# Hybrid DeltaNet and Conformer trunk: filling units, the split of u and gated products at the end of the delta stage

## Chip, core and metric

The kernel runs on one core of a Trainium2 chip. The metric is the device time of one execution in microseconds (us). Engines are named as in the profile: PE (TensorE, matrix products), PEld (its weight loads), DVE (VectorE), ACT (ScalarE), POOL (GpSimd) and SP (SyncE, which here only issues DMAs). Each engine takes its instructions strictly in the order in which they stand in its queue.

## What is computed

Two layers of a sequence model on x of shape 1 x 2048 x 1024. Cut to what matters here, each layer does this:

```
h    = rms_norm(x)
proj = h @ w_in                      # q, k, v, z_a, a, b, cf_val, cf_glu, z_b, gate logits
o    = gated delta rule, chunked, forwards and backwards over the sequence (q, k, v, decay, beta)
y_a  = (norm(o) * silu(z_a)) @ w_dn_out
u    = silu(layer_norm(conv31(cf_val * sigmoid(cf_glu)))) * silu(z_b)
y_b  = u @ w_cf_out
gate = sigmoid(gate_logits + gate_b)          # one 1024-wide gate for each branch
x    = x + (gate[0] * y_a + gate[1] * y_b) @ w_out
```

## The kernel before

Tokens lie along the free axis, channels on the partitions. Every dense product is made of fp32 values split in a high and a low half (`split`: ACT copies the high half, DVE subtracts it to get the low half), so one step over 128 input channels is three matmuls of 128x512 (L174, L175, L176). Call these three a **unit**. Weights are loaded by SP (`wraw`) and split in the same way (`whi`, `wlo`).

A layer has three parts. First come the projections, the convolutions and everything else that needs only h. Then comes the **delta stage** (`delta`): 16 steps, each of which advances the forward and the backward recurrence by one chunk of 128 tokens. Its products are small and each depends on the last, so between them `pull(n)` puts n units of work that does not depend on the recurrence, taken from the generator `filler`: 32 groups of 8 units that make the gate logits of the second half of the sequence (`gates(1)`), and then 64 units, in 16 groups of 4, that make y_b for the first half (`early_merge`). That is 320 units. `LEAD` says how many are pulled before step 0, `STEP` how many at the four places of a step, `TAIL` how many at three places after the last step; what is left then runs with nothing between. Then comes the **merge** (`merge`): for each half of the sequence, 8 channel tiles j by 2 token blocks b, the gated sum of both branches and then the product with w_out.

Within a step, in written order: L967 and L970 (key and query against the state, forward lane, then backward lane), L972 (DVE) and L976 (ACT), pull, L983, L985 (ACT), pull, L992 and L1001, the state update L995 and the output L1003 (both DVE), pull, `finish` of the previous pair of chunks, pull. `finish` (from step 8 on) normalises two output chunks: squares L1022 on ACT, a chain of tiny DVE operations that ends with L1036, the scaling L1040 on ACT, four transposes for each chunk on PE (L1045), L1046 on DVE, and the store to `og`. `prep` prepares the small triangular inverses of later steps (L895 to L950). PSUM tiles called pz come from a ring of five, those called pd (dense products) from a ring of three: who wants one waits until its last user is done.

Within the delta stage the order on PE, ACT, DVE and POOL is the written one (`bind`). Elsewhere, and on SP, a scheduler places instructions, and it also brings some of the merge's first work forward into the end of the delta stage.

u is loaded when unit 239 is done (8 loads, in the low halves' place), and split into its halves at the units that `SPLITS` names. The merge of the first half waits for the last `finish`: its `og` goes to DRAM, comes back as `gop`, and is split.

Of the kernel before, what the change touches and what calls it, by code (L numbers as in the profile page):

```python
# [6 lines left out]
F32 = mybir.dt.float32  # L7
F32R = mybir.dt.float32r
I32 = mybir.dt.int32
AF = mybir.ActivationFunctionType  # L10
ALU = mybir.AluOpType
# [3 lines left out]
P = 128  # L15
L = 2048
HALF = 1024
NB = 512
D = 1024
KD = 8  # L20
# [5 lines left out]
R1 = 3.0  # L26
R3 = 4.5
GAP = 0
SPLITS = [250, 251, 252, 253]
LEAD = (8, 10, 6, 6, 6, 4)  # L30
STEP = (5, 4, 4, 4)
TAIL = (3, 3, 3)
Z = '121'
LATE = 4
AHEAD = 4
# [22 lines left out]
def sort(ps):  # L58
    return ps.rearrange("p (i a) -> p a i", a=2)


def cut(x):
    return x.rearrange("p (a i) -> p a i", a=2)
# [13 lines left out]
class Trunk:  # L77
# [734 lines left out]
    def delta(self):  # L812
# [240 lines left out]
        def pull(n):  # L1053
            for _ in range(n):
                if next(fill, GAP) == GAP:
                    return
# [28 lines left out]
        for step in range(NCH):  # L1085
# [12 lines left out]
            next(last)  # L1098
            pull(STEP[0])
            for x in lanes:  # L1100
# [3 lines left out]
            go(step + 1)  # L1104
            pull(STEP[1])
            for x in lanes:
# [6 lines left out]
            next(new)  # L1113
            pull(STEP[2])
            next(last)
            ready = go(step + 1)
            last = new
            pull(STEP[3])
            ins = nxt
        for n in TAIL:  # L1120
            pull(n)
# [5 lines left out]
    def filler(self):  # L1127
        wcf = self.a["w_cf"][self.l]
        u = None
        for n, v in enumerate(self.gates(1)):  # L1130
            yield v
            if n == 30 * KD - 1:
                self.drain()
                self.rate = 0.0
                u = self.big([P, 8, HALF], F32R, "uop")
                raw = lambda k, b: u[:, 4 + k, b * NB:(b + 1) * NB]
                for b in range(2):
                    for k in range(4):
                        self.load(raw(k, b).bitcast(F32), self.u_d[k, :, b * NB:(b + 1) * NB])
            if n == 31 * KD - 1:  # L1140
                ahead = self.weight(wcf[0], 4)
            if n in SPLITS:
                k = SPLITS.index(n)
                self.split(u[:, k, 0:NB], raw(k, 0), raw(k, 0).bitcast(F32))
        self.u0 = u
        self.t1 = self.big([P, KD, HALF], F32, "t1")
        yield from self.early_merge(wcf, ahead, raw)

    def early_merge(self, wcf, ahead, raw):
        nc = self.nc  # L1150
        for j in range(KD):
            wc = ahead
            if j + 1 < KD:
                ahead = self.weight(wcf[j + 1], 4)
            for b in range(2):
                sl = slice(b * NB, (b + 1) * NB)
                ps = self.pd()
                for k, more in enumerate(self.dense_steps(ps, wc, lambda k: (self.u0[:, k, sl], self.u0[:, 4 + k, sl]), 4)):
                    if j == 0 and b == 0:
                        self.split(self.u0[:, k, NB:HALF], raw(k, 1), raw(k, 1).bitcast(F32))  # L1160
                    if more:
                        yield 1
                nc.scalar.activation(cut(self.t1[:, j, sl]), sort(ps), AF.Copy)
                yield 1

    def operand_parts(self, src, half, name):
        t = self.big([P, 8, HALF], F32R, name)
# [16 lines left out]
    def merge(self, l, xd, fnw):  # L1184
        nc, a = self.nc, self.a
        v_ = nc.vector
        last = l == self.depth - 1
        if not last:
            xnew = self.drm.tile([KD, P, L], F32, name=f"x{l + 1}")
            nvec = self.pv.tile([P, NV], F32, tag="vec", name="vec")  # L1190
            self.load(nvec, a["vecs"][l + 1])
        self.nh = [None] * 4
        prev = None
        wcol = lambda k: nvec[:, V_NW + k:V_NW + k + 1]
        for half in range(2):
            if half == 0:
                og, piece = self.operands(self.og_d, 0, "gop")
                for k in range(4):
                    piece(k)
            yhi = self.big([P, KD, HALF], F32R, "yhi")  # L1200
            ylo = self.big([P, KD, HALF], F32R, "ylo")
            for j in range(KD):
                wc = self.weight(a["w_cf"][l, j], 4) if half else None
                wd = self.weight(a["w_dn"][l, j], 4)
                for b in range(2):
                    sl = slice(b * NB, (b + 1) * NB)
                    tk = slice(half * HALF + b * NB, half * HALF + (b + 1) * NB)
                    gt = self.hm("gt")[:, 0:2 * NB].rearrange("p (n t) -> p n t", n=2)
                    self.load(gt, self.gt_d.rearrange("(n j) p t -> j p n t", n=2)[j][:, :, tk])
                    nc.scalar.activation(gt, gt, AF.Sigmoid)  # L1210
                    y = [gt[:, 0, :], gt[:, 1, :]]
                    if half:
                        ps = self.pd()
                        self.dense(ps, wc, lambda k: (u[:, k, sl], u[:, 4 + k, sl]), 4)
                        v_.tensor_tensor(out=cut(y[1]), in0=sort(ps), in1=cut(y[1]), op=ALU.mult)
                    else:
                        v_.tensor_tensor(out=y[1], in0=self.t1[:, j, sl], in1=y[1], op=ALU.mult)
                    ps = self.pd()
                    self.dense(ps, wd, lambda k: (og[:, k, sl], og[:, 4 + k, sl]), 4)
                    v_.tensor_tensor(out=cut(y[0]), in0=sort(ps), in1=cut(y[0]), op=ALU.mult)  # L1220
                    v_.tensor_tensor(out=y[0], in0=y[0], in1=y[1], op=ALU.add)
                    self.split(yhi[:, j, sl], ylo[:, j, sl], y[0])
            ahead = iter(())
            if half == 0:
                u, pu = self.operands(self.u_d, 1, "uop")
                og, pg = self.operands(self.og_d, 1, "gop")
                ahead = (f(k) for f in (pu, pg) for k in range(4))
            if last:
                self.last_out(l, half, xd, fnw, yhi, ylo, ahead)
                continue  # L1230
            w = self.weight(a["w_out"][l, 0], KD)
            norm = self.normalise(0, *prev, wcol) if prev is not None else iter(())
            xn = []
            for j in range(KD):
                next(ahead, None)
                if half and j == AHEAD:
                    self.scalar_weights(l + 1)
                for _ in range(2 if j % 2 == 0 else 0):
                    next(norm, None)
                if j < 6 and j % 2 == 0:  # L1240
                    t = self.mid("xn")
                    xn += [t[:, 0:HALF], t[:, HALF:2 * HALF]]
                elif j >= 6:
                    xn.append(self.hm("xnh")[:, 0:HALF])
                if j == 0:
                    ss = self.hm("ss")[:, 0:HALF]
                for b in range(2):
                    sl = slice(b * NB, (b + 1) * NB)
                    tk = slice(half * HALF + b * NB, half * HALF + (b + 1) * NB)
                    ps = self.pd()  # L1250
                    self.dense(ps, w, lambda k: (yhi[:, k, sl], ylo[:, k, sl]), KD)
                    xr = self.st("xr")
                    self.load(xr, xd[j][:, tk])
                    v_.tensor_tensor(out=cut(xn[j][:, sl]), in0=sort(ps), in1=cut(xr), op=ALU.add)
                    self.add_square(ss[:, sl], xn[j][:, sl], j == 0)
                    self.store(xnew[j, :, tk], xn[j][:, sl])
                if j + 1 < KD:
                    w = self.weight(a["w_out"][l, j + 1], KD)
            if half:
                continue  # L1260
            r = self.norm_stats(ss)
            prev = (xn, r)
        if last:
            return None, None
        self.ready = 2
        self.lead = self.late_norm(xn, ss, wcol)
        self.vec = nvec
        nh = self.nh
        return nh, [xnew[k] for k in range(KD)]
# [94 lines left out]
```

## Time and profile before

| | |
|---|---|
| device time, median of 3 runs | 3219.36 us (3217.04 to 3219.66) |
| the profiled execution's own time | 3223.96 us |
| its span in the trace | 3222.2 us |
| PE matmuls busy | 3101.0 us, 96% |
| DVE busy | 2401.9 us, 75% |
| ACT busy | 1393.5 us, 43% |
| POOL busy | 302.2 us, 9% |

The profiled execution was 4.6 us longer than the median of the runs, and 1.8 us of its time lie outside the span. The end of a matmul in the trace is modelled, and matmuls overlap, so that a busy PE may still be held up inside a group. The share is an average: where the remaining PE time is lost has to be looked up stage by stage. The delta stage of the first layer lies at about 900 to 1300 us, its merge of the first half behind it up to about 1365; in the second layer they lie at about 2475 to 2874 and 2883 to 2937.

### The profile page before, as it was taken

The numbers are of one execution on the slowest core, as the hardware profiler recorded it, in microseconds if no ns is written. First come the engines' busy times: TensorE is split into PE (matmuls) and PEld (weight loads), VectorE is DVE, ScalarE is ACT, GpSimd is POOL, SyncE is SP. The second block draws the span as 40 slices with busy tenths as digits, with TensorE's granted clock in tenths as the row PEclk, the third lists the DMA queues.
The fourth block names the chain that finished last, engine by engine and source line by source line (L and its number), as shares of the span: only waits on it lengthen the run. The fifth ranks groups of instructions, "written<-read, shape, count | busy, mean of one in ns | idle before, by whom it ended". The sixth has DMA issues, their size and how long they took to land. (4 is left out here: it accounts for less than half of the span.)

```text
span 3222.2 us, 51090 instructions
## 1 busy us (share of the span) xinstructions
PE 3101.0 (96%) x19110; PEld 2711.5 (84%) x19110; DVE 2401.9 (75%) x4409; ACT 1393.5 (43%) x3104; POOL 302.2 (9%) x297
## 2 busy tenths in 40 slices
PE   6999999999999999799999999999999999989997
PEld 5788888888889998687888888888888999877786
DVE  7789898987555687645666989898955567867655
ACT  5625252522344466533345242425234445655332
POOL 3000000000022231000000000000002122200000
PEclk9999999999999999899999999999999999999999
DMA  4233232334687785654413131314358777856644
GB/s 139 88 96 94 84 100 78 102 108 132 215 289 231 261 270 174 191 187 128 141 50 107 66 116 62 119 59 122 116 188 269 236 254 246 265 155 208 206 128 147
DMA packets 427030, 501.67 MB, mean 156 GB/s; under 512 B 95712, under 2 KB 260192, under 8 KB 426784
## 3 DMA queue, kind: packets, MB, share of 16 engines
q1 hardware_dynamic: 354032, 388.58, 38.9%
q10 hardware_dynamic: 64688, 80.09, 7.1%
q0 software_dynamic: 8064, 29.76, 2.4%
q8 instruction: 150, 2.46, 0.3%
q14 instruction: 96, 0.79, 0.1%
HBM read 342.74 MB, written 155.58 MB: 155 GB/s over the span
## 5 line engine op out<-in xcount | busy, mean ns | idle before, releaser
L174 PE MATMUL pd<-h,whi 128*128 128x512 f32 x2816 | 1091.7, 388 | 0.0
L176 PE MATMUL pd<-h,wlo 128*128 128x512 f32 x2816 | 1071.3, 380 | 2.3 <-DVE wlo L158 2.3
L175 PE MATMUL pd<-h,whi 128*128 128x512 f32 x2816 | 1072.1, 381 | 0.0
L728 DVE SCALAR_TENSOR_TENSOR cacc<-gp,vec,cacc 128x1009 f32<-128x1009 f32 (+1 forms) x480 | 615.5, 1282 | 37.8 <-ACT cacc L726 34.7
L174 PEld LDWEIGHTS pd<-h,whi 128*128 128x128 f32 x2816 | 534.6, 190 | 79.3 <-issue 1.4
L176 PEld LDWEIGHTS pd<-h,wlo 128*128 128x128 f32 x2816 | 534.4, 190 | 79.5 <-DVE wlo L158 3.9
L175 PEld LDWEIGHTS pd<-h,whi 128*128 128x128 f32 x2816 | 534.5, 190 | 72.9 <-issue 1.9
L157 ACT ACTIVATE whi<-wraw 128x512 fp32r<-128x512 f32 x400 | 243.0, 624 | 488.6 <-PE pd L175 346.6
L158 DVE TENSOR_TENSOR wlo<-wraw,whi 128x512 fp32r<-128x512 f32 x400 | 279.7, 713 | 175.8 <-ACT whi L157 163.9
L553 DVE SCALAR_TENSOR_TENSOR acc<-cin,vec,acc 128x1022 f32<-128x1022 f32 (+1 forms) x192 | 246.9, 1300 | 14.7 <-ACT acc L551 13.6
L176 PE MATMUL pd<-yhi,wlo 128*128 128x512 f32 x512 | 195.3, 381 | 8.0 <-DVE wlo L158 7.9
L174 PE MATMUL pd<-yhi,whi 128*128 128x512 f32 x512 | 194.7, 380 | 1.4 <-ACT whi L157 1.3
L175 PE MATMUL pd<-ylo,whi 128*128 128x512 f32 x512 | 194.0, 379 | 0.0
L808 ACT ACTIVATE go<-pd,vec 128x512 f32<-128x512 f32 x128 | 87.0, 680 | 133.2 <-PE pd L176 122.6
L529 ACT ACTIVATE cin<-pd 128x512 f32<-128x512 f32 x96 | 57.0, 593 | 156.3 <-PE pd L176 156.1
L174 PE MATMUL pd<-gop,whi 128*128 128x512 f32 x256 | 99.9, 392 | 20.5 <-ACT gop L157 19.3
L176 PEld LDWEIGHTS pd<-yhi,wlo 128*128 128x128 f32 x512 | 96.7, 189 | 25.6 <-DVE wlo L158 12.2
L174 PE MATMUL pd<-uop,whi 128*128 128x512 f32 x256 | 102.9, 402 | 12.8 <-ACT uop L157 7.1
L1210 ACT ACTIVATE gt<-gt 128x1024 f32<-128x1024 f32 x64 | 67.6, 1058 | 108.1 <-DMA gt<-gt 98.9
L740 ACT ACTIVATE ao<-pd 128x512 f32<-128x512 f32 x64 | 38.3, 598 | 170.0 <-PE pd L176 169.9
L976 ACT ACTIVATE dm<-pz,eg 128x128 f32<-128x128 f32 x240 | 68.5, 368 | 98.8 <-PE pz L970 93.7
L174 PEld LDWEIGHTS pd<-yhi,whi 128*128 128x128 f32 x512 | 96.8, 189 | 16.4 <-ACT whi L157 3.0
(296 smaller groups left out, 4837.0 us busy)
## 6 DMA issues: line engine op xcount, KB each, us to landing
wraw<-w_in SPq DMA_DIRECT2D x240, 256.0 KB, 3.2
gt<-go ACTq DMA_DIRECT2D x128, 256.0 KB, 3.4
dl<-gr SPq DMA_DIRECT2D x128, 256.0 KB, 5.1
dl<-kq SPq DMA_DIRECT2D x64, 512.0 KB, 5.9
dl<-kv SPq DMA_DIRECT2D x64, 512.0 KB, 5.2
gt<-gt SPq DMA_DIRECT2D x64, 512.0 KB, 5.0
wraw<-w_out SPq DMA_DIRECT2D x96, 256.0 KB, 3.0
kq<-acc SPq DMA_DIRECT2D x16, 1024.0 KB, 5.5
```

The source lines that it names most:

```text
L157: self.nc.scalar.activation(hi, src, AF.Copy)
L158: self.nc.vector.tensor_tensor(out=lo, in0=src, in1=hi.bitcast(F32), op=ALU.subtract)
L174: mm(ps, whi[:, k, :], xhi, start=k == 0, stop=False)
L175: mm(ps, whi[:, k, :], xlo, start=False, stop=False)
L176: mm(ps, wlo[:, k, :], xhi, start=False, stop=k == kk - 1)
L529: nc.scalar.activation(cut(t[:, o + b * NB:o + (b + 1) * NB]), sort(ps), AF.Copy)
L553: self.nc.vector.scalar_tensor_tensor(out=out, in0=t[:, k:k + n], scalar=wc(k), in1=out, op0=ALU.mult, op1=ALU.add)
L728: self.nc.vector.scalar_tensor_tensor(out=acc, in0=t[:, k:k + n], scalar=wc(k), in1=acc, op0=ALU.mult, op1=ALU.add)
L740: nc.scalar.activation(cut(o), sort(ps), func)
L808: nc.scalar.activation(cut(o), sort(ps), AF.Identity, bias=self.vec[:, V_GB + j:V_GB + j + 1])
L976: nc.scalar.activation(hv(o1)[:, hd, :], pq[:, hd, :], AF.Copy, scale=eg[:, hd:hd + 1])
L1210: nc.scalar.activation(gt, gt, AF.Sigmoid)
```

## The change

Three things. (1) A step pulls 16 units instead of 17 and the three places of TAIL 3, 3, 2, so that 16 units run after the last transposes. (2) u is split at units 247 to 254, one 512-wide piece at each, both token blocks; before, the first block was split at 250 to 253 and the second in the first group of `early_merge`. (3) `early_merge` no longer stores y_b alone (ACT copy, `t1`): it loads the gate of its own tile and block one group ahead, takes the sigmoid on ACT, and DVE writes gate times product to `y1`. The merge of the first half then loads one gate instead of two, and loses a DVE product for each tile and block.

```
-SPLITS = [250, 251, 252, 253]
+SPLIT = 247
-STEP = (5, 4, 4, 4)
-TAIL = (3, 3, 3)
+STEP = (4, 4, 4, 4)
+TAIL = (3, 3, 2)
...
-            if n in SPLITS:
-                k = SPLITS.index(n)
-                self.split(u[:, k, 0:NB], raw(k, 0), raw(k, 0).bitcast(F32))
+            if SPLIT <= n < SPLIT + 8:
+                b, k = divmod(n - SPLIT, 4)
+                self.split(u[:, k, b * NB:(b + 1) * NB], raw(k, b), raw(k, b).bitcast(F32))
...
+        def gate(i):
+            j, b = seq[i]
+            t = self.st("g1")
+            self.load(t, self.gt_d[8 + j][:, b * NB:(b + 1) * NB])
+            return t
+        nxt = gate(0)
+        for i, (j, b) in enumerate(seq):
...
+            g = nxt
+            if i + 1 < len(seq):
+                nxt = gate(i + 1)
+            nc.scalar.activation(g, g, AF.Sigmoid)
...
-                nc.scalar.activation(cut(self.t1[:, j, sl]), sort(ps), AF.Copy)
+            nc.vector.tensor_tensor(out=cut(self.y1[:, j, sl]), in0=sort(ps), in1=cut(g), op=ALU.mult)
...
-                    self.load(gt, self.gt_d.rearrange("(n j) p t -> j p n t", n=2)[j][:, :, tk])
-                    nc.scalar.activation(gt, gt, AF.Sigmoid)
-                    y = [gt[:, 0, :], gt[:, 1, :]]
+                    n = 1 + half
+                    self.load(gt[:, 0:n], self.gt_d.rearrange("(n j) p t -> j p n t", n=2)[j][:, 0:n, tk])
+                    nc.scalar.activation(gt[:, 0:n], gt[:, 0:n], AF.Sigmoid)
+                    y = [gt[:, 0, :], gt[:, 1, :] if half else self.y1[:, j, sl]]
...
-                    else:
-                        v_.tensor_tensor(out=y[1], in0=self.t1[:, j, sl], in1=y[1], op=ALU.mult)
```

The change moves instructions. On PE, at the end of the first layer's delta stage, the last transposes (L1045) stood directly ahead of the merge's first product on `gop`. Before:

```order
L174 MATMUL pd<-uop,whi 128x512
L175 MATMUL pd<-uop,whi 128x512
L176 MATMUL pd<-uop,wlo 128x512
L1045 MATMUL pz<-con,dm_6984 128x128 x8
L174 MATMUL pd<-gop,whi 128x512 x2
L175 MATMUL pd<-gop,whi 128x512
L176 MATMUL pd<-gop,wlo 128x512
```

Now sixteen units of `early_merge` stand between the two; the first of them:

```order
L174 MATMUL pd<-uop,whi 128x512
L175 MATMUL pd<-uop,whi 128x512
L176 MATMUL pd<-uop,wlo 128x512
L1045 MATMUL pz<-con,dm_6984 128x128 x8
L174 MATMUL pd<-uop,whi 128x512
L175 MATMUL pd<-uop,whi 128x512
L176 MATMUL pd<-uop,wlo 128x512
```

On ACT, where u's second block is split and the squares of `finish` stand (L1022, step 12 before). Before, half of the first block and the whole second block come behind the squares, and the product is copied by ACT (L1163):

```order
L157 ACTIVATE uop<-uop 128x512 x2
L941 ACTIVATE dh_6989<-pz 128x256
L903 ACTIVATE dh_6988<-dh_6987 32x4x32 x4
L1022 ACTIVATE junk,oss<-dm_6984 128x128 x4
L1022 ACTIVATE junk,oss<-dh_6985 128x128 x4
L157 ACTIVATE uop<-uop 128x512 x2
L808 ACTIVATE go<-pd,vec 128x512
L151 DMA gt_150<-go 128x512
L157 ACTIVATE whi<-wraw 128x512
L157 ACTIVATE uop<-uop 128x512 x4
L1163 ACTIVATE t_10818<-pd 128x512
```

Now, in step 13, all of u comes ahead of them, and behind them stand a weight's high half, a table load and the first two gates' sigmoids (L1167 of the new file):

```order
L157 ACTIVATE uop<-uop 128x512 x4
L808 ACTIVATE go<-pd,vec 128x512
L151 DMA gt_150<-go 128x512
L941 ACTIVATE dh_6989<-pz 128x256
L903 ACTIVATE dh_6988<-dh_6988 32x4x32 x4
L1022 ACTIVATE junk,oss<-dm_6984 128x128 x8
L157 ACTIVATE whi<-wraw 128x512
L1167 ACT_TABLE_LOAD
L1167 ACTIVATE g_11059<-g_11059 128x512
L1167 ACTIVATE g_11067<-g_11067 128x512
L976 ACTIVATE dm_6983<-pz,eg 128x128 x8
```

On DVE at the end of that step 13, the first gated product (L1173 of the new file) and a weight's low half now stand between `prep`'s last operation (L907) and `finish`'s L1046:

```order
L907 TENSOR_TENSOR dl_6981<-dl_6981,dm_6982 128x512 x2
L158 TENSOR_TENSOR wlo<-wraw,whi 128x512
L1173 TENSOR_TENSOR y_11058<-pd,g_11059 128x512
L1046 SCALAR_TENSOR_TENSOR dh_6985<-pz,vec,dh_6985 128x512
L1046 SCALAR_TENSOR_TENSOR dh_6986<-pz,vec,dh_6986 128x512
L949 COPY dl_6981<-pz 64x4x64
L950 COPY dl_6981<-pz 64x4x64
L1173 TENSOR_TENSOR y_11058<-pd,g_11067 128x512
L972 SCALAR_TENSOR_TENSOR dl_6980<-pz,neg,dl_6980 128x128 x8
```

In steps 9 to 11 the two low halves of a gate weight now stand at that place too, ahead of L1046, in every step. Before, they wandered through the step (17 units are not a multiple of 8) and stood behind L1046 in these steps.

## Rows read from the trace of the kernel before

**Rows 1.** Windows: PE, PEld, DVE, ACT, POOL busy, granted clock, DMA share, GB/s.

```profile
1216.60:1220.03 3.43, 0.01 (x2) 0.01 (x1) 2.07 (x5) 3.24 (x16) 0.00 (x0) 0.94 0.98 330
1220.03:1230.00 9.97, 9.97 (x75) 8.21 (x76) 9.04 (x20) 6.12 (x15) 1.27 (x1) 0.68 0.58 187
1300.20:1310.09 9.89, 0.01 (x1) 0.00 (x0) 1.71 (x4) 1.69 (x3) 0.00 (x0) 0.57 0.78 243
1310.09:1320.00 9.91, 9.87 (x33) 7.83 (x34) 7.95 (x9) 6.33 (x7) 0.00 (x0) 0.74 0.43 168
2873.85:2883.30 9.45, 0.01 (x1) 0.01 (x1) 1.54 (x4) 1.67 (x3) 0.00 (x0) 0.74 0.83 256
2883.30:2893.30 10.00, 9.96 (x33) 7.86 (x34) 7.82 (x9) 6.25 (x7) 0.00 (x0) 0.73 0.41 154
2790.90:2794.64 3.74, 0.02 (x2) 0.01 (x1) 2.38 (x5) 3.52 (x18) 0.00 (x0) 0.80 0.88 306
2794.64:2804.00 9.36, 9.36 (x75) 7.61 (x76) 8.45 (x19) 6.01 (x15) 1.22 (x1) 0.72 0.51 148
```

**Rows 2.** Waits of PE, 1311 to 1367 and 2884 to 2940: total us, times, longest.

```profile
PE pd L176 <- DVE wlo L158: 7.1, 3, 2.7
...
PE pd L176 <- DVE wlo L158: 4.0, 3, 1.8
```

**Rows 3.** Windows, step 10 of the first layer; columns as in group 1.

```profile
1147.13:1170.88 23.75, 23.75 (x252) 21.60 (x251) 21.98 (x54) 16.14 (x54) 6.99 (x6) 1.00 0.90 284
```

**Rows 4.** Timeline of PE, end of the delta stage: start, us, instruction, [idle, releaser].

```profile
1289.63 0.60 PE L1045 MATMUL pz<-con,dh 128*128 128x128 f32 x4
...
1298.27 1.94 PE L1045 MATMUL pz<-con,dm 128*128 128x128 f32 x8
1310.09 1.22 PE L174 MATMUL pd<-gop,whi 128*128 128x512 f32 x2 [9.88 <-ACT gop L157]
```

**Rows 5.** Timeline of ACT and DVE, same stretch.

```profile
1297.38 2.45 ACT L1040 ACTIVATE dm<-dm,orr 128x128 f32<-128x128 f32 x8 [0.90 <-DVE orr L1036]
...
1308.98 1.06 ACT L157 ACTIVATE gop<-gop 128x1024 fp32r<-128x1024 f32 x1 [8.15 <-DMA gop<-og]
...
1310.07 5.04 DVE L158 TENSOR_TENSOR gop<-gop 128x1024 fp32r<-128x1024 f32 x4 [7.86 <-ACT gop L157]
```

**Rows 6.** Timeline of DVE, ACT and PE, step 10 (starts at 1147.13).

```profile
1158.96 0.28 DVE L929 COPY dh<-pz 32x128 f32<-32x128 f32 x1
...
1164.16 0.49 DVE L895 STREAM_TRANSPOSE dh<-dh 128x128 f32<-128x128 f32 x2
...
1168.31 1.40 DVE L1046 SCALAR_TENSOR_TENSOR dh<-pz,vec,dh 128x512 f32<-128x512 f32 x2
...
1164.49 1.26 ACT L903 ACTIVATE dh<-dh 32x128 f32<-32x128 f32 x4
...
1169.14 0.69 ACT L808 ACTIVATE go<-pd,vec 128x512 f32<-128x512 f32 x1
...
1148.91 1.06 PE L967 MATMUL pz<-dh,dl 128*128 128x128 f32 x8
```

**Rows 7.** Timeline: DVE of step 14 (starts at 1249.17), PE of step 15.

```profile
1258.77 0.17 DVE L1036 TENSOR_TENSOR orr<-orr,cq 128x8 f32<-128x8 f32 x1
...
1275.62 1.16 PE L967 MATMUL pz<-dh,dl 128*128 128x128 f32 x8 [0.74 <-DVE dh L1046]
```

**Rows 8.** Timeline of ACT, first layer: u's second block, the sigmoid's table load.

```profile
1222.00 2.17 ACT L157 ACTIVATE uop<-uop 128x512 fp32r<-128x512 f32 x4
...
1270.53 1.28 ACT L1210 ACT_TABLE_LOAD   x1 [1.18 <-DMA gt<-gt]
```

**Rows 9.** Groups by form, DVE, 1316 to 1366: busy, mean ns, idle before.

```profile
L1220 DVE TENSOR_TENSOR gt<-pd,gt 128x512 f32<-128x512 f32 x16 | 10.9, 684 | 1.6 <-PE pd L176 1.6
...
L1217 DVE TENSOR_TENSOR gt<-t,gt 128x512 f32<-128x512 f32 x12 | 8.2, 686 | 4.0 <-ACT gt L1210 4.0
```

**Rows 10.** Waits of SP's queue, 1180 to 1320: total us, times, longest.

```profile
SPq L145 <- DVE wlo L158: 36.8, 7, 6.8
```

More of the change, by code (lines that the diff above doesn't have):

```diff
@@ L1141, in filler, with early_merge @@
                 ahead = self.weight(wcf[0], 4)
-            if n in SPLITS:
-                k = SPLITS.index(n)
-                self.split(u[:, k, 0:NB], raw(k, 0), raw(k, 0).bitcast(F32))
+            if SPLIT <= n < SPLIT + 8:
+                b, k = divmod(n - SPLIT, 4)
+                self.split(u[:, k, b * NB:(b + 1) * NB], raw(k, b), raw(k, b).bitcast(F32))
         self.u0 = u
-        self.t1 = self.big([P, KD, HALF], F32, "t1")
-        yield from self.early_merge(wcf, ahead, raw)
-    def early_merge(self, wcf, ahead, raw):
+        self.y1 = self.big([P, KD, HALF], F32, "y1")
+        yield from self.early_merge(wcf, ahead)
+    def early_merge(self, wcf, ahead):
         nc = self.nc
[L1151 to L1162, printed above, removed]
-                nc.scalar.activation(cut(self.t1[:, j, sl]), sort(ps), AF.Copy)
-                yield 1
+        seq = [(j, b) for j in range(KD) for b in range(2)]
+        def gate(i):
[5 more added lines that the diff above has]
+        for i, (j, b) in enumerate(seq):
+            if b == 0:
+                wc = ahead
+                if j + 1 < KD:
+                    ahead = self.weight(wcf[j + 1], 4)
+            g = nxt
+            if i + 1 < len(seq):
+                nxt = gate(i + 1)
+            nc.scalar.activation(g, g, AF.Sigmoid)
+            sl = slice(b * NB, (b + 1) * NB)
+            ps = self.pd()
+            for more in self.dense_steps(ps, wc, lambda k: (self.u0[:, k, sl], self.u0[:, 4 + k, sl]), 4):
+                if more:
+                    yield 1
+            nc.vector.tensor_tensor(out=cut(self.y1[:, j, sl]), in0=sort(ps), in1=cut(g), op=ALU.mult)
+            yield 1
     def operand_parts(self, src, half, name):
```

## The prediction

> **What bounds the kernel now.** I read PE first, stage by stage, because only its losses can be given back. In the delta stage and at its end it has two holes in each layer [rows 1]. The first, of 3.43 and 3.74 us, is the wait for u's high half at the first units of `early_merge`. The second, of 9.89 and 9.45 us, lies behind the last unit: og is stored, loaded and split with nothing for PE to do. [...] So u costs 3.43 + 3.2 + 3.74 + 2.6 = 13.0 us, og 9.89 + 2.6 + 9.45 + 2.7 = 24.6 us. In the merge of the first half PE waits 7.1 and 4.0 us for DVE's low halves of weights [rows 2]; that is a third thing, 11.1 us. Between these places PE does not stop: step 10 takes 23.75 us and PE is busy for all of it [rows 3]. So the recurrence is hidden under the units, and the stage is as long as its PE work. The second point to see there is DVE, busy for 21.98 of the 23.75 us: the stage has little room on it.
>
> **Sixteen units at the end.** Twelve units and one group of eight transposes lie between the two L1045 rows, 8.64 us apart [rows 4]. With 0.87 for the transposes a unit is 0.647 us. Sixteen units are 10.35 us a layer, as long as the hole. They leave the 16 steps, one each, so a step becomes 23.75 - 0.65 = 23.1 us, if PE stays the bound. What is late next is the split of gop. With P = 1289.63, the first L1045 row of step 15:
>
> - The transposes of the last pair begin at P + 8.6. They wait for L1040, which was already held up 0.90 us by L1036 [rows 5]. Two products on DVE and their sigmoids on ACT now stand ahead of this chain, so I take it and the rest of `finish` 1.0 us later.
> - gop's first piece reached ACT at 1308.98 = P + 19.35, so now P + 20.3; its high half is ready at P + 21.4.
> - PE is through the transposes at about P + 12.0, and through the 16 units at P + 22.4. The hole is closed.
> - But the four low halves, 5.04 us in a row before [rows 5], now have two gated products and a weight's low half between them, 3 x 0.6 more: the last ends at about P + 28, and the first product on gop at about P + 28.5, where PE alone would have needed 2.6 us from P + 22.4. So 3.5 us of pacing stay, and 1.0 at the transposes.
>
> I add 1.0 us for a lower clock during the pacing (bounds 0 and the 2.6 of rows 1). Left of the second hole: 5.5 us a layer, 11 in all, a gain of 24.6 - 11 = 13.6 us. Bounds: 8 (the chain 3 us later in each layer) and 22.
>
> **u in front of the squares.** The eight high halves now stand ahead of the squares, and the loads have 11 us. So PE will not wait for u. What is late next? I count step 13 from its first L967.
>
> - DVE's tiny operations end at 9.8, as in step 14 before (1258.94 against 1249.17) [rows 7]. New: a weight's low half and four of u, 5 x 0.6, to 12.9. From there L929 to the start of L895 took 5.2 us in step 10 (1158.96 to 1164.16 [rows 6]).
> - Four more low halves of u, 2.5 us, now stand between the two: L895 begins at 12.9 + 5.2 + 2.5 = 20.6 and ends, 0.49 later, at 21.1. In step 10 it began at 17.0 (1164.16 against 1147.13).
> - ACT has done u's second block by then (four in 2.17 us [rows 8]) and now waits for L895. L903 and the squares take 4.65 (1164.49 to 1169.14 [rows 6]): 25.8. The weight's high half 0.6, the table load 1.28 [rows 8], the sigmoid 0.6: 28.3.
> - DVE waits there, because the first gated product stands ahead of L1046: product to 29.0, first L1046 to 29.7.
> - PE wants the second L967 of step 14 at 23.1 + 1.8 = 24.9 (1148.91 against 1147.13 [rows 6]). It takes the PSUM tile that the first L1046 frees; in step 15 it waits there already, 0.74 us [rows 7].
>
> So a new hole of 4.8 us opens in step 14 of each layer, longer than the one that closes, and by the two u holes of rows 1 the clock behind it costs 2.6 to 3.2, say 2.9. That is 7.7 a layer, 15.4 in all against 13.0: u's move **loses** 2.4 us. Bounds: a gain of 13 (no hole) and a loss of 9 (3 us more in each, with its clock).
>
> [...]
>
> **Weights' low halves ahead of L1046 (steps 9 to 11).** From L929 to L1046 DVE takes 9.35 us without a pause [rows 6]. A shorter step takes 0.65 of the 1.77 us that DVE had idle [rows 3]. The weight's high half comes behind the squares on ACT, where L808 begins in rows 6 (1169.14, 22.0 of the step), and ends 0.6 later; with a little for the handover two low halves run from 22.8 to 24.1, and the first L1046 to 24.7: PE wants it at 24.9. It just fits. I take 0.3 us a step, 1.8 us in all; bounds 0 and 1.5 a step, 9 us.
>
> **Gated products.** On ACT a sigmoid replaces a copy of the same shape, at nothing: ACT has idle time at these places. On DVE 16 products a layer, 16 x 0.68 = 11 us, come into steps 13 to 15 and the end. PE hides them, but for the place above; if that cover were gone they would cost 22 us. In the merge 16 products a layer of 0.686 us go [rows 9]. There DVE did for each tile and block four operations and half a weight's low half, 4.5 x 0.685 = 3.1 us, against PE's four units, 2.6 us. Now it is 3.5 x 0.685 = 2.4, less than PE. So most of the 11.1 us of rows 2 should go; I take 8 (bounds 3 and 13, the latter with clock). Half of the gates' loads move into the delta stage; these queue on SP (rivals).
>
> [...]
>
> **The sum.** 13.6 - 2.4 - 1.8 + 8 = 17.4 us off. The profiled execution took 3223.96 us, so 3206.6 by its own time; it was 4.6 us above the median, so **3202 us** against 3219.36.
>
> **Rivals.**
> - *No new hole.* If the gate's sigmoid or the squares come 5 us earlier than I count, step 14 runs through. For it: DVE has 1.77 us idle in a step, and my ledger adds up ten durations. Against it: the order on both engines. 3202 - 15.4 = 3187 us.
> - *The end does not cover.* The change would then not do what it says: og's store waits longer, since gate loads stand between za, og and gop in SP's queue, and DVE's lag holds PE in steps 9 to 11. Tail gain 8 instead of 13.6, steps 9 instead of 1.8: 3202 + 12.8 = 3215 us. For it: L1036 was late already [rows 5]. Against: the loads have several us.
> - *Gates late (slower).* SP waits for DVE to free raw weights, 36.8 us in 7 waits, one of 6.8 [rows 10]. Gate loads stand behind these weight loads; a late gate stops the product on DVE, behind it L1046, and with it PE. If that happens in steps 14, 15 and at the end, not only once as counted, it is two more holes of 7.7 us a layer: 3202 + 31 = 3233 us. It decides from (17.4 + 6.4) / 4 = 6 us a place. Against it: from gate 3 on each load is issued a group or more ahead.
>
> **How the numbers follow.** My forecast has 0.50, between 3193 and 3211 us; no new hole 0.22, about 3182 to 3193; the end does not cover 0.22, 3209 to 3224; gates late 0.06. A measurement of this kernel tells about 0.2%, 6.4 us, from no change: faster is below 3212.9. Of the third case two thirds lie above that, so same is 0.15; of the fourth most is slower, 0.05; faster 0.80. The range of 8 in 10 is 3183 to 3215 us: it takes in nearly all of the second case and half of the third.
>
> **What would show it.** After: PE busy in the 10 us behind the last L1045, then short waits for gop's low halves (right), or still a hole above 4 us (wrong). No wait for uop, but one of 3 to 7 us of PE at L967 for L1046 in step 14, with a fall of the clock behind it. Steps 1 to 8 of 22.2 us instead of 22.9, and steps 9 to 11 of 23.1 to 23.5. PE waits for wlo in the merge under 3 us in all. I am wrong if step 14 runs through, or if several steps show the wait for L1046.

## The result and the profile after

The changed kernel takes 3192.41 us (median of 4 runs, 3187.47 to 3194.28) against 3218.2 of the kernel before (4 runs): ratio 0.9918 [0.9901, 0.9935], 25.8 us less. I had forecast 17.4 less and 3202 us. The profiled execution took 3187.47 us, the shortest of the four; its span is 3185.7.

The waits of PE in the changed kernel, from step 13 to the first product on `gop`, and in the merge behind it, first layer (columns as in group 2):

```profile
PE pz L967 <- DVE dh L1046: 4.2, 1, 4.2
PE pd L174 <- ACT whi L157: 1.1, 1, 1.1
PE pz L1045 <- ACT dm L1040: 1.1, 1, 1.1
PE pd L175 <- DVE gop L158: 0.5, 1, 0.5
```

```profile
PE pd L175 <- DVE gop L158: 1.2, 2, 0.8
PE pd L174 <- ACT gop L157: 1.0, 1, 1.0
```

Both holes of [rows 1] are gone, and of the wlo waits of the merge [rows 2] none is left in this layer. The new hole is where the prediction put it: the second L967 of step 14 waits for L1046. Windows of the changed kernel (columns as in group 1): step 10; the hole and the 10 us behind it, in both layers.

```profile
1135.77:1158.87 23.10, 23.10 (x249) 21.03 (x248) 21.01 (x55) 15.22 (x52) 7.00 (x6) 1.00 0.87 272
1230.69:1234.92 4.23, 0.01 (x1) 0.00 (x0) 2.09 (x4) 4.20 (x10) 0.00 (x0) 0.96 0.52 177
1234.92:1244.92 10.00, 10.00 (x129) 9.24 (x130) 9.54 (x28) 4.29 (x13) 4.54 (x4) 0.85 0.56 159
2786.34:2790.57 4.23, 0.00 (x2) 0.00 (x1) 2.10 (x4) 4.20 (x10) 0.00 (x0) 1.00 0.31 103
2790.57:2800.57 10.00, 10.00 (x129) 9.12 (x130) 9.54 (x28) 4.26 (x13) 4.55 (x4) 0.83 0.53 159
```

Step 10 is one unit shorter than in [rows 3]. The hole is 4.23 us twice (4.8 forecast); the clock behind it (0.85 and 0.83 over 10 us) costs 1.5 to 1.7 us by the estimate (1 - clock) x window, where I took 2.9.

**Where the time went.** The starts of a few PE instructions cut the trace into stages. For kernels with 16 units a step I add the moved units, 0.647 us each (6 a layer to steps 9 to 14), or take them off (15 a layer from the next stage), so that only losses differ. "Merge" runs from the first product on `gop` to the first on `yhi`, "w_out" from there to the first product on the second half's u. Sums of both layers, in us; experiments are below:

| kernel | steps 9 to 14 | step 15 to gop | merge | w_out | sum |
|---|---|---|---|---|---|
| before | 298.9 | 73.4 | 98.5 | 180.3 | 651.1 |
| before, second profile | 299.3 | 73.3 | 98.2 | 181.7 | 652.5 |
| changed | 298.1 | 60.5 | 88.7 | 173.5 | 620.8 |
| changed, second profile | 298.1 | 58.3 | 90.2 | 173.1 | 619.7 |
| units_only | 301.1 | 53.2 | 99.0 | 178.9 | 632.2 |
| gated_only | 303.5 | 76.9 | 89.4 | 176.4 | 646.2 |
| units_gated | 305.5 | 58.8 | 89.4 | 173.2 | 626.9 |
| units_split | 291.2 | 52.8 | 100.7 | 178.5 | 623.2 |
| place_5425 | 306.2 | 52.3 | 87.8 | 174.5 | 620.8 |
| late_y0 | 291.2 | 60.3 | 91.8 | 173.9 | 617.2 |
| early_gate | 291.6 | 61.8 | 88.3 | 173.6 | 615.3 |
| best | 287.1 | 61.9 | 89.4 | 173.0 | 611.4 |
| us_late | 287.1 | 53.2 | 99.7 | 179.0 | 619.0 |
| best2 | 287.1 | 60.3 | 85.6 | 173.1 | 606.1 |

By these stages the changed kernel gains 0.8 + 12.9 + 9.8 + 6.8 = 30.3 us. Steps 1 to 8 agree in all profiles (366.1 us with their units), and two profiles of one kernel differ by 1.1 and 1.4 us in the sum, in a single column by up to 2.2. What is left of the span (projections, second half) no edit touches; it lies between 2197 and 2205 us. It goes with the execution and not with the edit: 2197.4 in late_y0, 2198.8 and 2198.7 in the changed kernel, where the profiled execution was 3.8, 4.9 and 6.8 us below its kernel's median, but 2205.4 in place_5425 and 2205.0 in the kernel before, where it was 2.6 and 4.6 above.

### The profile page after: what moved, and what is told of

Same layout as the page of the kernel before. It is cut to its first block, busy times and chain, and to the rows that moved or that the text cites. A ratio compares the mean times of both kernels' runs of the same rounds, so it can differ in the third digit from the quotient of the medians.

```text
span 3185.7 us, 51259 instructions
## 1 busy us (share of the span) xinstructions
PE 3090.6 (97%) x19110; PEld 2705.8 (85%) x19110; DVE 2398.4 (75%) x4409; ACT 1385.3 (43%) x3104; POOL 302.3 (9%) x297
## 5 line engine op out<-in xcount | busy, mean ns | idle before, releaser
L553 DVE SCALAR_TENSOR_TENSOR acc<-cin,vec,acc 128x1022 f32<-128x1022 f32 (+1 forms) x192 | 246.5, 1299 | 14.4 <-ACT acc L551 13.2
L175 PEld LDWEIGHTS pd<-ylo,whi 128*128 128x128 f32 x512 | 96.8, 189 | 13.6
L176 PE MATMUL pd<-uop,wlo 128*128 128x512 f32 x256 | 99.1, 387 | 2.3 <-DVE wlo L158 1.4
```

Of the source, the lines that this page charges most:

```text
L175: mm(ps, whi[:, k, :], xlo, start=False, stop=False)
L176: mm(ps, wlo[:, k, :], xhi, start=False, stop=k == kk - 1)
L553: self.nc.vector.scalar_tensor_tensor(out=out, in0=t[:, k:k + n], scalar=wc(k), in1=out, op0=ALU.mult, op1=ALU.add)
```

## Experiments

The first three do one part alone or undo one; each is timed against the kernel before on its own chip.

**units_only**: the kernel before with

```
-STEP = (5, 4, 4, 4)
-TAIL = (3, 3, 3)
+STEP = (4, 4, 4, 4)
+TAIL = (3, 3, 2)
```

> The kernel before with the first part alone: steps of 16 units, 16 units behind the last transposes; u's split and the products as before. Theory: each part pays at its own place. The hole before gop (9.89 and 9.45 us) closes but for some 2 to 3 us of pacing and the lower clock behind it goes, 16 us together; the wlo waits of the merge (7.1 and 4.0) stay; u's second block still stands behind the squares, so a hole of 4 to 5 us in step 13 stays in each layer, about what it was. 3203 us, 3198 to 3208. Rival, that the end is paced by DVE: without the gated products the low halves of gop and of the weights come late for the merge as well, the closed hole comes back as waits there, wlo waits of the merge above 20 us in all, 3211 us or more.

Measured 3203.4 us, ratio 0.9957 [0.9945, 0.997], 13.2 less. The end gained 20.2 us in the table, the whole hole. But the merge did not get shorter, although the lower clock behind the hole (5.3 us estimated from [rows 1]) is gone. The merge of both layers in the kernel before, then here, behind the line of its first 10 us:

```profile
1310.09:1361.24 51.15, 46.18 (x192) 38.73 (x193) 41.51 (x64) 28.67 (x38) 0.00 (x0) 0.92 0.58 176
...
2883.30:2930.62 47.32, 44.90 (x193) 37.81 (x194) 42.07 (x65) 29.23 (x38) 0.00 (x0) 0.94 0.57 188
```

```profile
1295.44:1305.44 10.00, 9.16 (x39) 6.86 (x38) 9.27 (x12) 6.59 (x10) 0.00 (x0) 1.00 0.55 195
```

```profile
1295.44:1346.88 51.44, 45.72 (x194) 36.67 (x193) 43.82 (x68) 29.19 (x41) 0.00 (x0) 0.97 0.63 188
...
2855.37:2902.97 47.60, 43.91 (x193) 35.29 (x191) 40.89 (x65) 28.16 (x40) 0.00 (x0) 1.00 0.61 193
```

DVE is busy for 43.8 of the 51.4 us and PE for 45.7: neither fills the stage, and each has waits for the other and for ACT (more on this in the next section). Of the rival this much is right: what a faster PE gains there is waited away. Its sign, wlo waits of the merge above 20 us, did not come. The u hole grew, to 5.4 us.

**gated_only**: the kernel before with the third part's edits, u split as before.

> The kernel before with the third part alone: gates taken in early_merge, products stored gated, one DVE product less in the merge of the first half; 17 units a step and the old split of u. Theory: the wlo waits of the merge of the first half and of its product with w_out fall under 3 us a layer, 11 to 14 us off; u's second block now stands behind a table load and a sigmoid on ACT, 1.9 us later in each layer, so its hole is 5.3 instead of 3.4 us, and 4 us are given back; the gop hole stays at 9 to 10 us. 3209 us, 3204 to 3213. Rival, that the merge is bound by PE and the wait only moves (to yhi, to the gates' loads): 3217 us or more, with waits of the merge of 8 us or more under other names.

Measured 3215.99 us, ratio 0.9996 [0.9986, 1.0006]: no change. The theory was right in the merge (9.1 and 3.9 us less), but steps 9 to 14 and the end gave back 8.0. That leaves 5.0 by the stages of one profile, 0.6 by the medians. Waits of PE in the first layer's steps and end:

```profile
PE pd L174 <- ACT gop L157: 10.4, 1, 10.4
PE pd L174 <- ACT uop L157: 4.8, 2, 3.4
PE pz L1045 <- ACT dm L1040: 1.0, 1, 1.0
PE pd L174 <- ACT whi L157: 0.5, 1, 0.5
```

The wait for u is longer, as foreseen; the wait for the last L1040 and the longer one for `gop` fit the gates' work on ACT and DVE in front of `finish`, which the expectation had not priced.

**units_gated**: the changed kernel with u's split put back (`SPLITS = [250, 251, 252, 253]`, the second block in the first group of `early_merge`).

> The changed kernel with u split at the old places: the second part undone. My prediction had u's move cost 2.4 us; the stage lengths of the two profiles say that it gave 2. Theory from the profiles: u's high halves now come behind squares, table load and first sigmoid, 6.5 us late for the first unit on the second block, then the first gated product and L1046 behind u's low halves; a hole of 6 to 8 us with its clock of 2 in step 13 or 14, against 6.0 a layer in the changed kernel. 2 to 5 us a layer more than the changed kernel: 3198 us, 3195 to 3202. Rival, the prediction's own step: u's move gives nothing or loses, 3188 to 3193 us.

Measured 3198.05 us, ratio 0.9944 [0.9929, 0.9958]. The wait for u is 7.34 us in one piece, with the clock at 0.76 over the 10 us behind it. Against the changed kernel steps 9 to 14 lose 7.4 us; so u's move gains, and my rival falls.

**place_5425**: the changed kernel with

```
-STEP = (4, 4, 4, 4)
+STEP = (5, 4, 2, 5)
```

> The changed kernel with the same 16 units a step laid out as 5, 4, 2, 5 instead of 4, 4, 4, 4. The first gated product is then issued behind L1046 on DVE, and the high half of the weight and the first sigmoid ahead of the squares on ACT; the work is the same to the instruction. Theory: the hole of 4.23 us in step 14 is made by the order alone (the product that waits for squares, table load and sigmoid, ahead of L1046). It goes to under 1 us with the lower clock behind it, 6.0 us a layer: 3181 us, 3177 to 3185. Rival: the hole is made by DVE's lateness (u's eight low halves in front of L895), which stays: L1046 comes within 1 us of where it was, 3189 to 3194 us. A second rival: fewer units between the output and L1046 leave another link of the recurrence bare, in all steps 9 to 15, 3192 us or more.

Measured 3191.47 us, ratio 0.9917 [0.9901, 0.9933]: not faster, as both rivals said. In the first layer's steps 9 to 14 PE now waits at

```profile
PE pz L947 <- ACT dh L941: 2.4, 1, 2.4
PE pz L1045 <- DVE dh L995: 2.1, 3, 1.5
PE pz L967 <- DVE dh L1046: 1.6, 3, 0.5
```

L941 stands behind a sigmoid that waited 3.42 us for its gate's DMA, L995 behind u's low halves. The new places of the pulls moved the weight's split, u's low halves and the first sigmoid too. Steps 10 and 11 take 24.44 us instead of 23.11 and 23.29, as the second rival foresaw. Step 14 does run through, in 23.11 us, but step 13 ahead of it takes 30.10 and is late itself, so the run does not decide about L1046.

**units_split**: the changed kernel without the third part (the kernel before with the first two).

> The changed kernel without its third part: 16 units a step, u in front of the squares, but the products stored ungated by ACT and multiplied in the merge as before. Theory: the hole of step 14 is the sum of what stands ahead of L1046 on DVE: the weight's low half (whose high half comes behind the squares) and the first gated product (behind table load and sigmoid). Without the product the first L1046 ends 1.9 us earlier: hole 2.3 instead of 4.23 us in each layer. The merge waits for wlo return, so that merge and w_out product of the first half take as long as in the run with the first part alone (278 us in both layers, 16 more than in the changed kernel). Against that run u gives 8 us, of the 7 to 8 that each u hole cost there: 3195 us, 3191 to 3200. Rival: the hole comes from u's low halves alone, 4 us or more also here, 3199 to 3204.

Measured 3193.4 us, ratio 0.9922 [0.9909, 0.9934]. The hole and the 10 us behind it, first layer:

```profile
1232.40:1234.69 2.29, 0.00 (x1) 0.00 (x0) 1.41 (x3) 2.29 (x8) 0.00 (x0) 1.00 0.24 92
1234.69:1244.69 10.00, 10.00 (x136) 9.06 (x137) 9.47 (x29) 5.41 (x17) 4.54 (x4) 1.00 0.48 133
```

The hole is 2.29 us, as the theory had it: nearly half of the 4.23 is the gated product's, and behind the shorter hole the clock does not fall at all. By the medians this kernel is as fast as the changed one: of the three parts two carry the gain.

**late_y0** and **early_gate**: the changed kernel with the first product issued one unit later (behind L1046), and with the first gate's sigmoid ahead of L941 (`n` counts units in `filler`):

```
+            if i == 0:
+                yield 1
             nc.vector.tensor_tensor(out=cut(self.y1[:, j, sl]), in0=sort(ps), in1=cut(g), op=ALU.mult)
-            yield 1
+            if i:
+                yield 1
```

```
+            if n == SPLIT - 4:
+                self.g0 = self.st("g1")
+                self.load(self.g0, self.gt_d[8][:, 0:NB])
+            if n == SPLIT + 7:
+                self.nc.scalar.activation(self.g0, self.g0, AF.Sigmoid)
...
-        nxt = gate(0)
+        nxt = self.g0
...
-            nc.scalar.activation(g, g, AF.Sigmoid)
+            if i:
+                nc.scalar.activation(g, g, AF.Sigmoid)
```

> The changed kernel with one instruction moved: the first gated product is issued one unit later, behind both L1046 on DVE; everything else in the order of the changed kernel. Theory (order on DVE): the hole at L967 of step 14 shrinks by what L1046 waited for the sigmoid, from 4.23 to 2.3 us, a step 14 of 26.3 instead of 29.1 us; 5 us in both layers, 3188 us, 3184 to 3191. Rival: the two products in a row delay L972 as much as L1046 gains, the wait goes to L983 and the step is 28.5 us or more, 3190 to 3195 us.

> The changed kernel with the first gate loaded twelve units earlier and its sigmoid (with the table load) ahead of L941 in step 13, where ACT has 3.2 us idle waiting for L895; DVE's order as in the changed kernel. Theory: the first product no longer waits for ACT, only the weight's low half does (its high half behind the squares): first L1046 ends 1.3 us earlier, hole 2.9 instead of 4.23 us, 3189 us, 3185 to 3192. Rival: L941 comes 1.9 us later and PE wants it after 2.4, so a gate 0.6 us late costs it again; then a wait at L947 and 3191 us or more.

Measured 3186.21 us, ratio 0.9901 [0.9886, 0.9915], and 3184.51, 0.9896 [0.9882, 0.991]. With the product behind L1046 the hole is 2.30 us and step 14 takes 25.67, as in units_split; the products do not hold L972. With the sigmoid early it is 2.44, and PE waits for another link:

```profile
PE pz L967 <- ACT dm L976: 2.4, 1, 2.4
```

L976 stands on ACT behind the weight's high half and the second gate's sigmoid. The size fits the theory, the releaser does not; L947 did not wait.

**best**: both edits, and the first early weight split with the second block:

```
             if b == 0:
                 wc = ahead
-                if j + 1 < KD:
-                    ahead = self.weight(wcf[j + 1], 4)
+            if b == int(j == 0) and j + 1 < KD:
+                ahead = self.weight(wcf[j + 1], 4)
```

> The changed kernel with nothing ahead of L1046 in step 13 that waits for ACT: the first gate early as in the run before, the first product behind L1046, and the first early weight split four units later, behind L1046 too. Theory: L1046 follows L907 at once, first one done 0.2 us after PE wants it: hole under 0.5 us, no lower clock, step 14 of 23.1 to 23.8 us: 11 us off the changed kernel, 3181 us, 3177 to 3185. Rival: two products and a low half in a row then make L972 late and the recurrence waits at L983, 2 us or more with a lower clock, 3186 us or more.

Measured 3180.49 us, ratio 0.9884 [0.9868, 0.99]; step 14 takes 23.59 us. The theory of the order on DVE holds to half a microsecond.

**us_late**: units_split with this last edit. **best2**: best, with each gate loaded two groups ahead (`gs` begins as `[self.g0, gate(1)]`) and its sigmoid issued after the second unit of the group before:

```
-            g = nxt
-            if i + 1 < len(seq):
-                nxt = gate(i + 1)
+            g = gs[i]
+            if i + 2 < len(seq):
+                gs.append(gate(i + 2))
...
+                if k == 1 and i + 1 < len(seq):
+                    nc.scalar.activation(gs[i + 1], gs[i + 1], AF.Sigmoid)
```

**after_again** is the changed kernel once more.

> The run without gated products, with the first early weight split four units later, so that its low half stands behind L1046 in step 13. Theory: then nothing that waits for ACT is ahead of L1046, the hole of 2.29 us closes to under 0.5 us, step 14 takes 23.1 to 23.6 instead of 25.66 us; the merge keeps its 279 us. 4 to 5 us off the run without gated products: 3189 us, 3185 to 3192. Rival: L907 itself ends too late (24.5 us into the step, when PE wants the tile at 25.1), 1 us or more stays, 3190 to 3195 us. Beside the kernel with everything mended (3180.5) it shows what the gated products are worth once their stalls in step 14 are gone: 8 us by the theory.

> The mended kernel with each gate loaded two groups ahead and its sigmoid issued two units earlier, so that at the end no product on DVE waits for a sigmoid that stands behind L1040 on ACT. Theory: the 4.1 and 3.6 us that a product waited in step 15, ahead of L1003, go; the squares, the weight's high half, L1046 and the last L1040 come as much earlier, and PE's waits for whi and L1040 at the end (1.5 and 1.1 us, and the clock behind them) go. Step 15 with the end 27.5 to 29 instead of 30 to 33 us by the count without the moved units, 6 to 8 us in both layers: 3174 us, 3170 to 3178. Rival: ACT itself is the bound there (the merge's first sigmoid waits 2 to 3.5 us for its gate's DMA in front of L985), the product's wait is only replaced, 3178 to 3184 us.

> The changed kernel itself once more, beside the next two on one chip, to see which stage lengths repeat. If the stages are what the theory takes them for, steps 9 to 14 again take 149.0 us in each layer, step 15 with the end 30 to 32 us by the count that leaves the moved units out, the merge of the first half with its product 261 to 263 us in both layers; what differs from the first profile lies in the projections. Median 3192 us, 3188 to 3196.

On one chip: us_late 3187.59 us, 0.9907 [0.9892, 0.9921]; best2 3175.07, 0.9871 [0.9855, 0.9888]; the changed kernel 3192.99, 0.992 [0.9906, 0.9935]. us_late is as its theory said. best2 beats both kernels, the changed one by 17.9 us, and its time lies in the range of its theory. But at the end it gained 1.6 of the 6 to 8 us against best; 3.8 stand in the merge column, where two profiles of one kernel differ by up to 1.5; what made them is not shown. Waits in the first layer's end, changed kernel and then best2:

```profile
ACT g L1167 <- DMA g<-gt: 4.7, 2, 2.9
DVE y L1173 <- ACT g L1167: 4.4, 1, 4.4
ACT gt L1221 <- DMA gt<-gt: 4.3, 2, 3.5
...
ACT junk L1022 <- DVE dm L1003: 2.0, 1, 2.0
...
PE pz L1045 <- ACT dm L1040: 1.1, 1, 1.1
```

```profile
ACT g L1176 <- DMA g<-gt: 6.1, 3, 3.4
...
PE pz L1045 <- ACT dm L1040: 3.0, 1, 3.0
```

The product's wait for its sigmoid, and with it the squares' wait for L1003, are gone, and ACT waits longer for the gates' DMA, in front of the last L1040: that is the rival's mechanism.

In after_again steps 9 to 14 repeat to 0.1 us; step 15 with the end takes 29.7 and 28.6 us by the count without the moved units, where I expected 30 to 32, and merge with w_out 263.3 in both layers, where I expected 261 to 263.

**before_again**: the kernel before, profiled once more.

> The kernel before, profiled once more. The two profiles of before and after differ by 36.5 us of span, their medians by 25.8 and 27.6 us. By the stages that the change touches (first step to the end of the first half's merge, both layers) they differ by 29.1 us, in the rest, which no edit touches, by 7.4. Theory: the rest varies from run to run and the touched stages do not, as they did not in two profiles of the changed kernel (988.1 and 987.0 us): again 1015 to 1018 us there, with holes of 3.4, 3.7, 9.9 and 9.4 us within 0.3. Rival: the touched stages of the first profile were long by chance, by 3 us or more, in the merge where weights come by DMA: 1014 us or less.

One run, 3223.09 us; the sum of the table's stages is 652.5 against 651.1 us, with steps 1 to 8 1018.6, where 1015 to 1018 was expected. The touched stages repeat, and the rival (3 us less) falls. So the stages say 30 to 33 us for the change and the medians 25.8 and 27.6; where the 3 to 7 us between them lie stays open.

## Why the prediction came out as it did

The direction and the range held; the gain was too small by 8.4 us, and three terms were mis-sized, in part against each other.

- **Merge: the term that failed.** I took 8 us, sized by the labelled waits of [rows 2]. The two columns merge and w_out fell by 16.6, in both pairs of profiles; against the same kernel without gated products (units_split) by 17.0. The waits that have a name are not the loss. In the first layer's merge of units_only, 51.44 us long, they are

```profile
PE pd L176 <- DVE wlo L158: 4.2, 3, 2.7
PE pd L175 <- DVE gop L158: 0.8, 2, 0.5
PE pd L174 <- ACT whi L157: 0.6, 2, 0.3
```

5.6 us together. But the changed kernel's PE needs 42.52 us for the same products, so 8.9 us are lost. The other 3.2 are in a PE busy time stretched to 45.72; up to 1.5 of them, an estimate, are the clock, 0.97 over the whole stage.

```profile
1297.17:1342.31 45.14, 42.52 (x194) 35.96 (x192) 38.43 (x59) 25.26 (x40) 0.00 (x0) 1.00 0.53 174
```

My own sentence on DVE, 3.1 us a tile and block against PE's 2.6, would have given 16 us for 16 of them in two layers. That this is near 16.6 is chance: it speaks of the merge alone, which gave 9.8, and its price is too high. It adds up durations, but in a row these operations start 0.60 us apart (units_only):

```profile
1322.22 0.68 DVE L1220 TENSOR_TENSOR gt<-pd,gt 128x512 f32<-128x512 f32 x1
1322.82 0.68 DVE L158 TENSOR_TENSOR ylo<-gt,yhi 128x512 fp32r<-128x512 f32 x1
1323.42 0.68 DVE L1221 TENSOR_TENSOR gt<-gt 128x512 f32<-128x512 f32 x1
```

So DVE needs 4.5 x 0.60 = 2.7 us a tile, about 43 us for the sixteen, hardly more than PE's 42.52. The 51.4 us are longer than the work of either. DVE is idle for 7.6 of them, and half of that is a wait for the sigmoids of the gates, which wait on ACT for their loads:

```profile
DVE gt L1217 <- ACT gt L1210: 3.9, 6, 1.7
```

```profile
ACT gt L1210 <- DMA gt<-gt: 13.8, 11, 3.2
```

Gated products take a DVE product, half of each sigmoid and half of each gate's load out of the merge at once. That the three together shorten it is shown; which of them does is not, because no run does one alone. Of the 6.8 us in w_out, the 2.5 of the first layer are not the gated products': w_out takes 83.69 us there in every run but the two of the kernel before. Why is open.

- **Sixteen units at the end: 13.6 forecast.** That was 17.3 up to the first product on `gop`, plus the clock, less the pacing behind. The clock's part is 2.6 and 2.7 us, estimated as (1 - clock) x window from 0.74 over 9.91 us and 0.73 over 10.00 [rows 1]; that it costs so much no run shows (below). The hole itself closed as worked out, and the pacing by gop's halves is 2.7 us in the first layer, where I took 3.5. But the column fell by 12.9 only, where units_only gained 20.2: the gated products cost 7.6 us here (against units_split; 5.5 in the changed kernel's second profile). I had put their cost at 1.0 us a layer. On DVE and ACT in step 15:

```profile
1266.77 0.68 DVE L1173 TENSOR_TENSOR y<-pd,g 128x512 f32<-128x512 f32 x1
1271.82 0.69 DVE L1173 TENSOR_TENSOR y<-pd,g 128x512 f32<-128x512 f32 x1 [4.37 <-ACT g L1167]
1272.43 1.28 DVE L1003 TENSOR_TENSOR dm<-pz,dm 128x512 f32<-128x512 f32 x2
```

```profile
1267.33 0.63 ACT L1221 ACTIVATE gt<-gt 128x512 f32<-128x512 f32 x1 [3.52 <-DMA gt<-gt]
...
1271.16 0.63 ACT L1167 ACTIVATE g<-g 128x512 f32<-128x512 f32 x1
```

The second product waits 4.37 us for a sigmoid behind both L1040, which stand behind the merge's first sigmoid (L1221), and that one waits for its gate's load. L1003, the squares and the last pair's chain wait with the product. This is my rival of the late gate, at one place and off PE's path for most of it: PE waits 1.1 us each for whi and L1040. In the second layer the clock behind them is 0.83 over 10 us, by the estimate another 1.7 us. The 5.3 us of clock in my term were no gain either: in units_only the merge has the full clock in its first 10 us, where the kernel before had 0.74, and is no shorter.

- **u's move: a loss of 2.4 forecast, a gain found.** The ledger of step 13 came out nearly to the microsecond. DVE and ACT, changed kernel (the step starts at 1205.64):

```profile
1212.53 0.17 DVE L1036 TENSOR_TENSOR orr<-orr,cq 128x8 f32<-128x8 f32 x1
...
1220.18 2.50 DVE L158 TENSOR_TENSOR uop<-uop 128x512 fp32r<-128x512 f32 x4 [2.66 <-ACT uop L157]
...
1225.97 0.50 DVE L895 STREAM_TRANSPOSE dh<-dh 128x128 f32<-128x128 f32 x2
...
1231.58 0.69 DVE L158 TENSOR_TENSOR wlo<-wraw,whi 128x512 fp32r<-128x512 f32 x1 [1.39 <-ACT whi L157]
1233.52 0.69 DVE L1173 TENSOR_TENSOR y<-pd,g 128x512 f32<-128x512 f32 x1 [1.25 <-ACT g L1167]
1234.13 1.40 DVE L1046 SCALAR_TENSOR_TENSOR dh<-pz,vec,dh 128x512 f32<-128x512 f32 x2
```

```profile
1230.93 0.61 ACT L157 ACTIVATE whi<-wraw 128x512 fp32r<-128x512 f32 x1
1231.56 1.28 ACT L1167 ACT_TABLE_LOAD   x1
1232.86 1.15 ACT L1167 ACTIVATE g<-g 128x512 f32<-128x512 f32 x2
```

L895 begins at 20.3 of the step (20.6 forecast), the product ends at 28.6 (29.0). Two errors cancelled on the way: L1036 was 2.7 us earlier than I took it, and DVE then stood 2.66 us for u's second block, which ACT copies behind L1040. What failed is the account: I set the whole new hole against u. Of its 6.0 us in a layer (29.06 - 23.11) units_split, which moves u as well, has 2.55; the other 3.4 are the gated product's. On the kernel with shorter steps u's move gains 9.9 us in steps 9 to 14 (units_only to units_split). In the 13.0 us that I took for the old holes 3.2 and 2.6 are the clock, by the same estimate from 0.68 over 9.97 us and 0.72 over 9.36 [rows 1], and the 2.9 behind each new one follow them; no run shows such a cost apart from its hole. Behind the new ones the estimate gives 1.5 and 1.7.

- **Steps 1 to 8** take 22.23 us, as forecast. **Steps 9 to 13:** 23.11, 23.11, 23.29, 23.48 and 23.11 us: 0.55 late a layer, 1.1 in both, where I took 1.8. The weight's low halves just fit.

- **Gated products as a whole** take 17.0 us out of the merge and w_out and put 6.9 into steps 9 to 14 and 7.6 into the end: 2.5 us by the stages, nothing by the medians (3193.4 without, 3192.4 and 3193.0 with them). The prediction had them at nothing on ACT and hidden on DVE, but for step 13 and 1.0 us a layer at the end. Their worth shows once their stalls are mended: us_late 3187.6, best2 3175.1.

## What to carry to other kernels

Work that is moved off a bound engine into a stage with slack keeps its place in the queues: list what each moved instruction waits for and what stands behind it, for every one of them, not only the first (here the first product behind L1046 instead of ahead of it made the hole 2.30 us instead of 4.23). Price a stage by its length against what its busiest engine needs for the work, not by the waits that the profile can name (51.44 us against 42.52, with 5.6 named); take an engine's pace from the starts of its operations in a row, not from their durations (0.60 us apart on DVE, 0.68 long); and count a faster clock or a closed hole only where PE sets the pace (the merge took 51.15 us at a clock of 0.92 and 51.44 at 0.97). The sum of the touched stages repeats to about 1 us here and a single stage to 2, where whole times scatter by 5 to 17.

## What the hardware showed unasked

- The granted clock behind a hole of PE in these stages: 1.00 behind 2.29 and 2.30 us, 0.85 and 0.83 behind 4.23, 0.79 behind 5.39, 0.76 behind 7.34 (means over 10 us each; the 0.85 is 0.50 from 1234.92 to 1238.00 and 1.00 from there to 1244.92). Closing half of the hole of step 14 gave back all of the clock. But the length of a hole does not decide it alone: behind 3.43 us it was 0.68 [rows 1], and behind the 1.1 us that PE waits for the last L1040 in the changed kernel it is 1.00 in the first layer and 0.83 in the second:

```profile
2839.75:2849.75 10.00, 10.00 (x37) 7.67 (x38) 4.15 (x8) 4.93 (x12) 0.00 (x0) 0.83 0.83 255
1284.59:1294.59 10.00, 10.00 (x45) 7.95 (x46) 4.76 (x8) 4.93 (x12) 0.00 (x0) 1.00 0.91 281
```

- The table load took 1.28 us, as in [rows 8], and nothing beside it shows: in the rows above ACT, busy with a copy just ahead, went from the high half (ends 1231.54) to the load and on to the sigmoid with 0.02 us on either side.
- A gated product that reads PSUM on DVE takes 687 ns (15 of them), the sum in the merge that reads SBUF 684; in [rows 9] it is 684 from PSUM and 686 from SBUF. Where the operand lies does not show in these durations.
